# Moving small transfers of the projection to GpSimd's queue and queueing two jobs later in a hybrid attention / gMLP layer

## The chip, the core and the metric

The kernel runs on one core of a Trainium2 chip. The core has a matrix engine (TensorE, PE in the profile; its weight loads are PEld), a vector engine (VectorE, DVE), an activation engine (ScalarE, ACT), a general engine (GpSimd, POOL) and SyncE (SP), which here only issues transfers. Each engine takes its instructions in order, and engines wait for one another by semaphores. A transfer (DMA) is issued by an engine, stands in that engine's queue until its own conditions hold, and is then carried by 16 transfer engines that all queues share. The metric is the device time of one execution in microseconds (us).

## The reference

One layer for 2048 latent tokens and 256 context tokens, width 1024, all in float32. The part that matters here is the input projection and what is made of it:

```python
h_x = modulate(x, norm1_g[l], sh1, sc1)
p_x = h_x @ w_in[l]
k_x = apply_rope(rmsnorm(kv_heads(p_x[..., :K_W]), k_norm_g[l]), cos, sin)
v_x = kv_heads(p_x[..., K_W:KV_COLS])
q_x, u_x, vg_x, ga_x, gb_x = jnp.split(p_x[..., KV_COLS:], REST_SPLITS, axis=-1)
q_x = apply_rope(rmsnorm(q_heads(q_x), q_norm_g[l]), cos, sin) * q_scale
...
attn_x = merge_heads(attend_blocked(q_x, k_all, v_all))
gm_x = gmlp_spatial(jax.nn.gelu(u_x), jax.nn.gelu(vg_x), gm_norm_g[l], gm_ws[l], gm_bs[l])
x = x + g1 * branch_merge(attn_x, gm_x, ga_x, gb_x, w_br_attn[l], w_br_gm[l], w_out[l])
h2 = modulate(x, norm2_g[l], sh2, sc2)
x = x + g2 * sq_relu_mlp(h2, w_ff1[l], w_ff2[l])
```

The gMLP mixes 128-token chunks: `gmlp_spatial` normalizes v, multiplies each chunk by a 128 x 128 matrix per head group, adds a bias and multiplies by u.

## The kernel before

**Products.** Every float32 operand is split into a high part and a remainder (`split`, `operand`, `pair_chunk`): ScalarE casts the high part, VectorE subtracts. A product is three matmuls, high x high, high x low, low x high (lines L1742 to L1744). The large products are done with seven block products instead of eight, numbered p and taken in the order `SUMS = (0, 1, 5, 6, 4, 2, 3)`. Each output block is complete after one of the passes 1, 4, 2 or 3.

**Stages.** Projection (`project`, roughly the first 740 us), attention, merging of the branches, and the feed-forward layer. Only the projection is touched. There, the 2048 tokens are worked in two blocks (`blk` 0 and 1) of two 512-token quarters each (`b` = 2 blk and 2 blk + 1). Within a block come two column groups called pairs, pair 0 (keys, values, queries; 2 x 384 columns) and pair 1 (the gMLP's u and v; 2 x 512 columns), and eight gate groups. In block 0 the order is pair 0, gate groups 0 and 1, pair 1, gate groups 2 to 7; in block 1 both pairs and then all gates. `pairs_run` works a pair in 14 steps: seven passes p with two chunks of weights each, and in each step four tiles of 128 tokens. Weights of a step are loaded, cast and subtracted up to three steps ahead (L694 from the weights, L710 and L712, L713 from the stored differences `t_d`).

**What a pair leaves.** `Pair.leave` (L2115) writes each 128-token tile of an output block to HBM (`p_d`). If the block is a plain copy, ScalarE copies and issues the store (L2119, L2123). If an earlier part has to be added, VectorE makes the sum (L2121) into a buffer tagged `t2`, of which there are six, and SyncE issues the store (L2123). That is so for the passes 4 and 2.

**Small jobs.** What becomes of `p_d` is done by generators in a list, `self.work`; each turn (`tick`) advances the first job of the list to its next `yield`, so that the instructions of a job are strewn between those of the products. A job waits in the list until those before it are done. The jobs are: `keys_work` (load from `p_d`, norm L779, L780, L810, table L465 to L480, rotation L491 to L498, split L820, L821, transposes L192, store to `k_d` L834), `queries_work` (the same for queries, loads L842 to L844, L851), `mixing` (the gMLP; loads L871 and L896, split L157, load of the transposed mixing matrices `ws_d` L919, products L186, result to `gm_d`), `gm_consts` (L954 to L960, which makes `ws_d`), `terms` (weight differences of pair 1) and `h_ahead` (operands of block 1). `mixing` takes buffers tagged `m`, of which there are four, so the buffer for `ws_d` is one that the split L157 has just read. In block 0, a steered generator (`opening`) also runs `context_keys` from step 10 of pair 0 on: load of the context (L505), sums of squares (L515), reciprocal root on VectorE (`rsqrt`, L163 to L179), scaling (L528), transposes (L999), modulation (L1003), and its own small product.

**Which job comes when.** `Pair.begin` has a table `ends`: after which pass which jobs are appended. For pair 0 these are the first keys after pass 1, the first queries after pass 2, and the second keys and queries after pass 3. In block 0 no job gets a turn before step 9 of pair 0, which is part of pass 4, since the operand sums go first (`hold`). `terms` is inserted behind the job that is first in the list when the first pair ends, and must be done early in the second.

**Order on the engines.** The framework's planner orders the instructions of each engine in the projection by its own estimates of durations and by what each depends on; some stretches are pinned to the written order (`order`). All the loads of weights, the stores named above except ScalarE's, and the loads of the jobs are on SyncE's queue.

Of the kernel before, what the change touches and what calls it, by code (L numbers as in the profile page):

```python
# [72 lines left out]
class Kern:  # L73
# [387 lines left out]
    def rope_tables(self, w, b):  # L461
        nc = self.nc
        H = HD // 2
        cs = self.t1([TT, HD])
        nc.sync.dma_start(  # L465
            cs, self.I["rope"].rearrange("(t p) d -> p t d", p=P)[:, b * TT : (b + 1) * TT]
        )
        gb = self.rg[w].unsqueeze(1).broadcast_to([P, TT, HD])
        tab = self.t2([2, TT, HD])
        t1, t2 = tab[:, 0], tab[:, 1]  # L470
        cos, sin = cs[:, :, :H], cs[:, :, H:]
        for o in (0, H):
            nc.vector.tensor_tensor(
                out=t1[:, :, o : o + H], in0=cos, in1=gb[:, :, o : o + H], op=ALU.mult
            )
        nc.vector.scalar_tensor_tensor(
            out=t2[:, :, :H], in0=sin, scalar=-1.0, in1=gb[:, :, H:],
            op0=ALU.mult, op1=ALU.mult,
        )
        nc.vector.tensor_tensor(out=t2[:, :, H:], in0=sin, in1=gb[:, :, :H], op=ALU.mult)  # L480
        return t1, t2
# [317 lines left out]
    def keys_work(self, nt, b, kraw=None):  # L799
        nc = self.nc  # L800
        c = 0 if b is None else b + 1
        if b is not None:
            kraw = self.t2([TT, NKV, HD])
            nc.sync.dma_start(
                kraw.rearrange("p t h d -> p t (h d)"), self.rows(self.pr_d[0][b][0], slice(0, P))
            )
            yield
            yield
# [18 lines left out]
        for kv in range(NKV):  # L827
            ps = self.bank([TB])
            self.transposes(
                ps, [f32(kk[:, t, kv]).rearrange("p a d -> p (a d)") for t in range(nt)]  # L830
            )
            ka = self.t2([TB])
            nc.scalar.copy(ka[:, :n], ps[:, :n])
            nc.sync.dma_start(self.k_d[c][kv][:, :n], ka[:, :n])  # L834
        yield

    def queries_work(self, b):
# [3 lines left out]
        src = self.pr_d[0][b]  # L841
        nc.sync.dma_start(flat[0][:, :, :P], self.rows(src[0], slice(2 * P, 3 * P)))  # L842
        nc.sync.dma_start(flat[0][:, :, P:], self.rows(src[1], slice(0, P)))
        nc.sync.dma_start(flat[1], self.rows(src[1], slice(P, 3 * P)))  # L844
        yield
# [23 lines left out]
    def raw_values(self, b, j, c):  # L869
        x = self.m4([TT, 4, HD])  # L870
        self.nc.sync.dma_start(  # L871
            x.rearrange("p t g d -> p t (g d)"),
# [19 lines left out]
    def mixing(self, b, c):  # L892
        nc = self.nc
        v, u = (self.raw_values(b, j, c) for j in range(2))
        gn = self.t2([256])
        nc.sync.dma_start(  # L896
            gn,
# [20 lines left out]
        ws = self.m4([2, 4, P], F32R)  # L918
        nc.sync.dma_start(f32(ws).rearrange("p n g q -> p n (g q)"), self.ws_d[c])  # L919
        yield  # L920
# [29 lines left out]
    def gm_consts(self):  # L950
        nc = self.nc
        for c in range(2):
            w = self.t2([4, P])
            nc.sync.dma_start(w, self.I["gm_ws"][0, c * 4 : (c + 1) * 4].rearrange("g p q -> p g q"))  # L954
            ps = self.bank([TB])
# [3 lines left out]
            nc.vector.tensor_tensor(out=t[:, 1], in0=ps, in1=f32(t[:, 0]), op=ALU.subtract)  # L959
            nc.sync.dma_start(self.ws_d[c], f32(t))  # L960
            yield
# [1131 lines left out]
class Pair:  # L2093
# [6 lines left out]
    def begin(self, blk):  # L2100
        self.blk = blk
        k, b = self.k, 2 * blk
        if self.index == 0:
            self.ends = {
                1: lambda: [k.keys_work(TT, b)],
                2: lambda: [k.queries_work(b)],
                3: lambda: [k.keys_work(TT, b + 1), k.queries_work(b + 1)],
            }
# [6 lines left out]
    def leave(self, i, j, t, ps, u=None):  # L2115
# [6 lines left out]
        dst = k.pr_d[self.index][2 * self.blk + i][j]  # L2122
        (nc.scalar if u is None else nc.sync).dma_start(dst[t * P : (t + 1) * P, :], x)  # L2123

# [304 lines left out]
```

## Time and profile before

| what | us |
|---|---|
| median of 3 runs | 3018.83 (3016.13 to 3022.55) |
| the profiled execution | 3009.05 |
| its span, first to last instruction | 3007.2 |
| TensorE's idle time in the span | 75.6 |

How to read the profile: the page gives the busy time of each engine and its share of the span. A stretch row gives the same in a window of time, with the share of full speed that TensorE's clock was granted and the busy share of the transfer engines. A wait row reads "engine, tile, line <- the engine, tile and line that released it: total us, times, longest us". In a timeline row stand the start, the duration, the engine, the line, the operation and its tiles, and in brackets the idle time before it and what ended it. "SPq" is SyncE issuing a transfer; such rows merge neighbours of one line (x2), and a merged row's duration runs from the first to the last. Tile names have their buffer numbers left out; `t` stands for `t1`, `t2` and `t4`, and `p_d<-t` is a store of a sum. Landing times of transfers are not in this trace.

### The profile page before, as it was taken

The numbers are of one execution on the slowest core, as the hardware profiler recorded it, in microseconds if no ns is written. First come the engines' busy times: TensorE is split into PE (matmuls) and PEld (weight loads), VectorE is DVE, ScalarE is ACT, GpSimd is POOL, SyncE is SP. The second block draws the span as 40 slices with busy tenths as digits, with TensorE's granted clock in tenths as the row PEclk, the third lists the DMA queues.
The fourth block names the chain that finished last, engine by engine and source line by source line (L and its number), as shares of the span: only waits on it lengthen the run. The fifth ranks groups of instructions, "written<-read, shape, count | busy, mean of one in ns | idle before, by whom it ended". The sixth has DMA issues, their size and how long they took to land. (4 is left out here: it accounts for less than half of the span.)

```text
span 3007.2 us, 37935 instructions
## 1 busy us (share of the span) xinstructions
PE 2931.6 (97%) x13325; PEld 2206.7 (73%) x13325; DVE 2062.5 (69%) x2983; ACT 1417.9 (47%) x2318; POOL 652.8 (22%) x470
## 2 busy tenths in 40 slices
PE   7899999989999999999999989999999999999999
PEld 5778788876555555556888878888887888888887
DVE  5866487765788888867555587776676766654555
ACT  5554865553544545444222354444454344444432
POOL 0000000001999899894211200000000000000000
PEclk9999999999999999999999999999999999999999
DMA  7587866774010010016776658888766544447564
GB/s 276 184 295 272 307 215 217 256 247 140 24 36 26 25 37 22 22 36 191 238 215 194 183 198 308 307 305 303 261 219 224 186 154 154 154 154 277 210 209 155
DMA packets 386175, 559.04 MB, mean 186 GB/s; under 512 B 38640, under 2 KB 192416, under 8 KB 385984
## 3 DMA queue, kind: packets, MB, share of 16 engines
q1 hardware_dynamic: 373616, 535.89, 53.7%
q10 hardware_dynamic: 12368, 20.73, 1.8%
q8 instruction: 105, 1.72, 0.2%
q14 instruction: 86, 0.70, 0.1%
HBM read 379.75 MB, written 176.69 MB: 185 GB/s over the span
## 5 line engine op out<-in xcount | busy, mean ns | idle before, releaser
L2251 DVE TENSOR_REDUCE ts<-b 128x1 f32<-128x512 f32 x512 | 313.0, 681 | 75.3 <-PE b L2240 75.2
L2336 POOL TENSOR_TENSOR ac<-ac,p 128x512 f32<-128x512 f32 x214 | 306.3, 1463 | 50.5 <-ACT p L2308 50.5
L1858 DVE TENSOR_TENSOR b<-b,b 128x1024 fp32r<-128x1024 f32 x170 | 200.7, 1220 | 135.7 <-ACT b L1857 135.4
L1857 ACT CAST b<-b 128x1024 fp32r<-128x1024 f32 x170 | 170.6, 1050 | 222.2 <-PE b L1744 100.1
L2308 ACT ACTIVATE p<-b 128x512 f32<-128x512 f32 x384 | 194.1, 627 | 168.6 <-PE b L2304 168.1
L1743 PE MATMUL b<-b,b 128*128 128x512 f32 x680 | 265.2, 390 | 2.8 <-DVE b L1858 2.7
L1742 PE MATMUL b<-b,b 128*128 128x512 f32 x680 | 266.0, 391 | 1.6 <-DVE f L1879 1.4
L1744 PE MATMUL b<-b,b 128*128 128x512 f32 x680 | 264.7, 389 | 0.0
L2336 POOL TENSOR_TENSOR ac<-p,p 128x512 f32<-128x512 f32 x32 | 52.4, 1656 | 746.0 <-DMA raw<-in_w_mod 741.3
L2336 POOL TENSOR_TENSOR ac<-ac,t 128x512 f32<-128x512 f32 x152 | 205.0, 1378 | 0.0
L2285 PE MATMUL b<-h,h 128*128 128x512 f32 x576 | 188.0, 406 | 3.9 <-ACT p L2308 2.2
L2316 PE MATMUL b<-p,h 128*64 128x512 f32 x768 | 186.5, 609 | 0.0
L2304 PE MATMUL b<-h,h 128*128 128x512 f32 x576 | 179.1, 392 | 0.0
L1743 PE MATMUL b<-hb,b 128*128 128x512 f32 x446 | 173.8, 390 | 0.0
L1752 DVE TENSOR_TENSOR f<-f,b 128x512 f32<-128x512 f32 x160 | 109.0, 682 | 78.6 <-issue 45.8
L1742 PE MATMUL b<-hb,b 128*128 128x512 f32 x415 | 162.0, 390 | 0.3 <-DVE f L1752 0.3
L1744 PE MATMUL b<-hb,b 128*128 128x512 f32 x415 | 161.3, 389 | 0.0
L2285 PEld LDWEIGHTS b<-h,h 128*128 128x128 f32 x576 | 104.1, 189 | 65.1 <-DVE ts L2251 26.0
L1743 PEld LDWEIGHTS b<-b,b 128*128 128x128 f32 x680 | 127.6, 188 | 31.4 <-DVE b L1858 4.7
L1742 PEld LDWEIGHTS b<-b,b 128*128 128x128 f32 x680 | 127.6, 188 | 29.5 <-ACT b L1857 2.3
L1744 PEld LDWEIGHTS b<-b,b 128*128 128x128 f32 x680 | 127.7, 188 | 26.4
L157 POOL TENSOR_TENSOR bw<-bw,bw 128x512 fp32r<-128x512 f32 x58 | 75.8, 1328 | 235.7 <-ACT bw L153 235.7
(436 smaller groups left out, 7207.0 us busy)
## 6 DMA issues: line engine op xcount, KB each, us to landing
ao_d<-f SPq DMA_DIRECT2D x224, 256.0 KB
f<-in_w_ff SPq DMA_DIRECT2D x48, 1024.0 KB
b<-ao_d SPq DMA_DIRECT2D x85, 512.0 KB
b<-w2o_d SPq DMA_DIRECT2D x85, 512.0 KB
w2o_d<-f SPq DMA_DIRECT2D x112, 256.0 KB
f<-in_w_in SPq DMA_DIRECT2D x38, 512.0 KB
f<-x_d SPq DMA_DIRECT2D x64, 256.0 KB
hb<-ao_d SPq DMA_DIRECT2D x54, 256.0 KB
```

Of the source, the lines that this page charges most:

```text
L1742: mm(ps, wh, hh, start=start and k == 0, stop=False, skip_group_check=True)
L1743: mm(ps, wh, hl, start=False, stop=False, skip_group_check=True)
L1744: mm(ps, wl, hh, start=False, stop=k == len(w) - 1, skip_group_check=True)
L1752: nc.vector.tensor_tensor(out=out, in0=in0, in1=in1, op=op)
L1857: nc.scalar.copy(h, f32(l))
L1858: nc.vector.tensor_tensor(out=l, in0=f32(l), in1=f32(h), op=ALU.subtract)
L2251: nc.vector.tensor_reduce(out=self.mx[:, t, h, c : c + 1], in_=ps[h], axis=AX.X, op=ALU.max)
L2285: self.nc.tensor.matmul(self.pts[j][h], k.KA[c][self.kv][:, ks], self.qa[h], start=True, stop=False, skip_group_check=True,)
L2304: self.nc.tensor.matmul(s, k.KB[c][self.kv][:, ks], self.qb[h], start=False, stop=True, skip_group_check=True,)
L2308: self.nc.scalar.activation(pt[h], s, AF.Exp)
L2316: nc.tensor.matmul(self.o[h * HD : (h + 1) * HD, :], k.V[c][:, i, self.kv * HD : (self.kv + 1) * HD], pt[h], start=j == 0, stop=j == NKT - 1,)
L2336: nc.gpsimd.tensor_tensor(out=self.acc[e][:, h], in0=old[:, h], in1=pt[h], op=ALU.add)
```

## The change

Twelve places that issued on SyncE's queue now issue on GpSimd's: the rotation table, the loads for keys, for queries, for u and v and for the gMLP's norm, the load of the mixing matrices, the stores of keys, the two transfers of `gm_consts`, and the stores of VectorE's sums. That is 102 transfers in an execution: 32 stores of sums, 10 of keys and 2 of mixing matrices, and 58 loads. No transfer was issued by GpSimd before.

The table `ends` of pair 0 is written from a list of four jobs and the passes after which they are appended. In block 1 these are the passes of before (1, 2, 3, 3); in block 0 they are (2, 3, 3, 3): the first keys are appended after pass 2 in place of pass 1 and the first queries after pass 3 in place of pass 2, which are steps 11 and 13 of the 14 (numbered from 0) in place of 3 and 11.

```diff
     def rope_tables(self, w, b):
...
-        nc.sync.dma_start(
+        nc.gpsimd.dma_start(
             cs, self.I["rope"].rearrange("(t p) d -> p t d", p=P)[:, b * TT : (b + 1) * TT]
         )
...
     def keys_work(self, nt, b, kraw=None):
...
-            nc.sync.dma_start(
+            nc.gpsimd.dma_start(
                 kraw.rearrange("p t h d -> p t (h d)"), self.rows(self.pr_d[0][b][0], slice(0, P))
             )
...
-            nc.sync.dma_start(self.k_d[c][kv][:, :n], ka[:, :n])
+            nc.gpsimd.dma_start(self.k_d[c][kv][:, :n], ka[:, :n])
...
     def queries_work(self, b):
...
-        nc.sync.dma_start(flat[0][:, :, :P], self.rows(src[0], slice(2 * P, 3 * P)))
-        nc.sync.dma_start(flat[0][:, :, P:], self.rows(src[1], slice(0, P)))
-        nc.sync.dma_start(flat[1], self.rows(src[1], slice(P, 3 * P)))
+        nc.gpsimd.dma_start(flat[0][:, :, :P], self.rows(src[0], slice(2 * P, 3 * P)))
+        nc.gpsimd.dma_start(flat[0][:, :, P:], self.rows(src[1], slice(0, P)))
+        nc.gpsimd.dma_start(flat[1], self.rows(src[1], slice(P, 3 * P)))
...
     def raw_values(self, b, j, c):
...
-        self.nc.sync.dma_start(
+        self.nc.gpsimd.dma_start(
             x.rearrange("p t g d -> p t (g d)"),
...
     def mixing(self, b, c):
...
-        nc.sync.dma_start(
+        nc.gpsimd.dma_start(
             gn,
...
-        nc.sync.dma_start(f32(ws).rearrange("p n g q -> p n (g q)"), self.ws_d[c])
+        nc.gpsimd.dma_start(f32(ws).rearrange("p n g q -> p n (g q)"), self.ws_d[c])
...
     def gm_consts(self):
...
-            nc.sync.dma_start(w, self.I["gm_ws"][0, c * 4 : (c + 1) * 4].rearrange("g p q -> p g q"))
+            nc.gpsimd.dma_start(w, self.I["gm_ws"][0, c * 4 : (c + 1) * 4].rearrange("g p q -> p g q"))
...
-            nc.sync.dma_start(self.ws_d[c], f32(t))
+            nc.gpsimd.dma_start(self.ws_d[c], f32(t))
...
         if self.index == 0:
+            at = (1, 2, 3, 3) if blk else (2, 3, 3, 3)
+            jobs = [w for c in (b, b + 1) for w in (k.keys_work(TT, c), k.queries_work(c))]
             self.ends = {
-                1: lambda: [k.keys_work(TT, b)],
-                2: lambda: [k.queries_work(b)],
-                3: lambda: [k.keys_work(TT, b + 1), k.queries_work(b + 1)],
+                p: lambda p=p: [w for q, w in zip(at, jobs) if q == p] for p in set(at)
             }
...
     def leave(self, i, j, t, ps, u=None):
...
-        (nc.scalar if u is None else nc.sync).dma_start(dst[t * P : (t + 1) * P, :], x)
+        (nc.scalar if u is None else nc.gpsimd).dma_start(dst[t * P : (t + 1) * P, :], x)
```

## The prediction

> **What bounds the kernel now.** I read the page first, then the busy time by stretches of 30 us in the stage that the change touches (the projection, the first 740 us), then TensorE's waits there, and last the timeline of the one long wait.
>
> ```profile
> span 3007.2 us, 37935 instructions
> PE 2931.6 (97%) x13325; PEld 2206.7 (73%) x13325; DVE 2062.5 (69%) x2983; ACT 1417.9 (47%) x2318; POOL 652.8 (22%) x470
> ```
>
> TensorE is busy 97% of the span, so the whole idle time is 3007.2 - 2931.6 = 75.6 us, and no change of queues can win more than its part of that. The stretches (columns: length, then busy us and instructions of PE, weight loads, DVE, ACT, POOL; then granted clock, DMA share, GB/s):
>
> ```profile
> 90.00:120.00 30.00, 19.71 (x102) 18.09 (x103) 23.97 (x61) 14.93 (x25) 0.00 (x0) 0.83 0.63 196
> 120.00:150.00 30.00, 30.00 (x163) 25.61 (x162) 26.27 (x46) 18.29 (x30) 0.00 (x0) 1.00 0.60 183
> 150.00:180.00 30.00, 28.65 (x133) 23.00 (x132) 18.36 (x25) 11.72 (x19) 0.00 (x0) 1.00 0.89 319
> 180.00:210.00 30.00, 28.46 (x132) 23.32 (x132) 15.77 (x45) 15.05 (x27) 0.00 (x0) 1.00 0.94 311
> ```
>
> The reader is to see three things: TensorE loses 30 - 19.71 = 10.3 us in one stretch and 0 to 1.5 us in those behind it; the granted clock is 0.83 in that stretch alone; and VectorE has 26.27 of 30 us of work right behind it, but 18.36 and 15.77 later. TensorE's waits (who, for whom: total us, times, longest), the first from the view of 75 to 150 us, the others from that of 117 to 740 us:
>
> ```profile
> PE b L999 <- ACT m L528: 6.9, 2, 6.4
> ...
> PE b L186 <- DMA m<-ws_d: 5.2, 6, 1.5
> PE a L1742 <- ACT a L2176: 4.5, 4, 1.9
> PE b L192 <- DVE m L821: 1.9, 2, 1.5
> PE a L1742 <- ACT t L2178: 1.6, 1, 1.6
> ```
>
> One wait of 6.4 us stands out, and the only transfer that TensorE itself waits for is the load of the mixing weights (ws_d). The timeline around the long wait:
>
> ```profile
> 99.88 0.19 ACT L515 ACTIVATION_READ_ACCUMULATOR t<-m 128x1 f32 x1
> 103.08 0.16 DVE L163 TENSOR_SCALAR ts<-ts 128x2 f32<-128x2 f32 x1
> 104.94 0.69 DVE L498 TENSOR_TENSOR t<-t,t 128x512 f32<-128x512 f32 x1
> 105.93 0.83 ACT L712 CAST f<-f 128x768 fp32r<-128x768 f32 x1 [5.86 <-DMA f<-t_d]
> 106.79 0.96 DVE L713 TENSOR_TENSOR f<-f,f 128x768 fp32r<-128x768 f32 x1 [1.16 <-ACT f L712]
> 108.84 0.16 DVE L179 SCALAR_TENSOR_TENSOR ts<-ts,ts 128x2 f32<-128x2 f32 x1
> 109.09 2.19 ACT L528 ACTIVATE m<-m,ts 128x1024 f32<-128x1024 f32 x2 [0.76 <-DVE ts L179]
> 110.30 0.48 PE L999 MATMUL b<-ident,m 128*128 128x128 f32 x1 [6.37 <-ACT m L528]
> 111.33 0.48 PE L999 MATMUL b<-ident,m 128*128 128x128 f32 x1 [0.56 <-ACT m L528]
> 112.52 0.69 PE L999 MATMUL b<-ident,m 128*128 128x128 f32 x2 [0.71 <-ACT t L1003]
> 114.29 0.69 PE L1742 MATMUL a<-f,hx 128*128 128x384 f32 x1 [1.09 <-ACT a L734]
> ```
>
> Read backwards: TensorE's transposes of the context (L999) wait for the scaling (L528), that for the last step of a reciprocal root on VectorE (L179). The sums of squares were ready at 99.88 + 0.19 = 100.07, but the root's first step (L163) came at 103.08 and its last at 108.84. Two things lie between. One is the first keys' job, whose rotation (L498) runs until 105.6. The other is VectorE's in-order wait at L713 for ScalarE's L712, which waits 5.86 us for a weight load (f<-t_d). That load is late because SyncE issues it late:
>
> ```profile
> 93.86 0.33 SPq L2123 DMA_DIRECT2D p_d<-t  x1
> ...
> 95.99 3.07 SPq L2123 DMA_DIRECT2D p_d<-t  x2
> 99.15 0.39 SPq L1047 DMA_DIRECT2D f<-in_w_in  x1
> 99.59 0.72 SPq L710 DMA_DIRECT2D f<-t_d  x1
> ```
>
> Between 95.99 and 99.06 its queue holds two stores of VectorE's sums (L2123), the second issued only when its sum is made; the loads behind it go out at once afterwards, so they were ready earlier. Both causes are just what the diff moves.
>
> **The change part by part.**
>
> *A, the long wait.* The keys' job of block 0 leaves this place: it is now queued after the pass p = 2 rather than p = 1. Counted by the loops, its first step moves from step 9 to step 11 of the first pair. Some of what VectorE sheds ahead of the root:
>
> ```profile
> L498 DVE TENSOR_TENSOR t<-t,t 128x512 f32<-128x512 f32 x1 | 0.7, 692 | 0.0
> L810 DVE TENSOR_TENSOR t<-t,ts 128x512 f32<-128x512 f32 x1 | 0.7, 683 | 0.0
> ...
> L780 DVE TENSOR_REDUCE ts<-m 128x8 f32<-128x512 f32 x1 | 0.7, 679 | 0.0
> ```
>
> That is 692 + 683 + 679 ns = 2.05 us, and the job's table, the rest of its rotation and its own root come on top. The root could then start near 100.1 rather than 103.1. The load f<-t_d goes out up to 99.06 - 95.99 = 3.1 us earlier, so L712 ends near 103.7 rather than 106.8 and L528 can follow at once. TensorE reaches L999 at 110.30 - 6.37 = 103.93, so most of the 6.37 us is gone: I keep 1.0 of it. Of the three small waits behind it (0.56 + 0.71 + 1.09 = 2.36 us) I keep half, since they come from ScalarE's and VectorE's alternation, which stays. The clock comes on top:
>
> ```profile
> 107.20:117.40 10.20, 4.75 (x15) 3.76 (x16) 8.03 (x19) 6.17 (x9) 0.00 (x0) 0.50 0.25 80
> ```
>
> It is at half speed for 10.2 us, beginning 3.3 us after the idle time began; 4.75 us of matmuls in it would take half as long at full speed, so 2.4 us. Sum of A: 5.4 + 1.2 + 2.4 = -9.0 us; bounds 0 (the load lands no earlier and takes the whole chain with it) to -(6.37 + 2.36 + 2.4) = -11.1.
>
> The Trainium skill's page "TensorE: Matmul & The Clock Gate" (Part 1) says that the gate knows half and full speed only and needs some 3.4 us of busy time to open again. The trace agrees on the two values; by that figure alone the clock would be worth about 1.7 us in place of 2.4, an estimate.
>
> *B, SyncE's queue.* 102 transfers leave it: 32 stores of sums, 12 of keys and mixing weights, and 58 loads for the small jobs. Its waits in the projection for two of them alone:
>
> ```profile
> SPq L2123 <- DVE t L2121: 41.4, 22, 6.4
> ...
> SPq L919 <- DVE m L157: 21.0, 8, 7.8
> ```
>
> Weight loads queued behind these go out earlier. But no wait of TensorE's beyond ws_d is for a transfer: weights are first cast by ScalarE, and what TensorE can feel of a late one is a wait for a ScalarE copy that stands behind the cast, L2176 and L2178 (4.5 + 1.6 = 6.1 us). I take half, -3.0; bounds 0 and -6.1.
>
> *C, the load of the mixing weights.* It cannot start before VectorE's L157 has freed a buffer, and TensorE waits for it:
>
> ```profile
> 444.43 1.22 DVE L157 TENSOR_TENSOR m<-m,m 128x1024 fp32r<-128x1024 f32 x1
> ...
> 445.68 0.32 SPq L919 DMA_DIRECT2D m<-ws_d  x1
> ...
> 449.66 0.38 PE L186 MATMUL b<-m,m 128*128 128x256 f32 x1 [0.90 <-DMA m<-ws_d]
> ```
>
> L157 ends at 445.65 and the issue follows in 0.03 us: SyncE's queue costs this load nothing, so GpSimd's can only be slower. From issue to use are 3.98 us. No transfer in this trace is issued by GpSimd, so its extra time is bounded by 0 and by half of those 3.98 us; I take 0.5, near the low end because the issue row itself is 0.32 us. With the 6 waits that are already exposed: +3.0 us, bounds 0 and +12.
>
> The Trainium skill's page "DMA: Bandwidth & Descriptors" (Specifications) gives about 1 us to the first byte from GpSimd's queue and 0.6 from SyncE's or ScalarE's. By it C would be 6 x 0.4 = 2.4 us, an estimate; no run here shows it yet.
>
> *D, the jobs in their new place.* The keys' job runs beside the last three steps of the first pair, and the queries' job of block 0 leaves the stretch 120:150 and comes behind the context's keys and the mixing constants, by the count of steps in 150:180 and 180:210. There VectorE has 11.6 and 14.2 idle us. From the pass p = 2 of the second pair on, nothing is late: in the kernel before, the loops' turns for jobs ran empty ahead of that point, and these turns take up the delay. I take one more wait of the kind L192 <- L821: +1.0, bounds 0 and +4. If VectorE were not idle there, the queries' full-width work would stand in line with the sums, and the upper bound would hold.
>
> *E, buffers.* Sums, keys and tables share six t2 buffers, which a store holds until it has landed. A slower store gives them back later: +1.0, with the upper end in the first rival.
>
> Sum: -9.0 - 3.0 + 3.0 + 1.0 + 1.0 = -7.0 us. The profiled execution took 3009.05 us (span 3007.2 and 1.85 around it), so 3002.0; the median of the runs shown is 9.8 us above it, and against that median the forecast is 3018.8 - 7.0 = **3011.8 us**.
>
> **The rivals.**
>
> *First, GpSimd's queue cannot keep up (slower).* The stores come in bursts:
>
> ```profile
> 435.06 0.89 SPq L2123 DMA_DIRECT2D p_d<-t  x2
> ...
> 446.14 0.81 SPq L2123 DMA_DIRECT2D p_d<-t  x2
> ```
>
> Eight of them lie between 435.06 and 446.95, 1.5 us apart. Six buffers cover some 6 x 1.5 = 9 us more. If one transfer occupies GpSimd's queue for over (11.9 + 9) / 8 = 2.6 us, VectorE waits for a buffer, TensorE's bank is not emptied, and TensorE waits. At 3.2 us, 8 x 3.2 - 20.9 = 4.7 us in each of four bursts: +19, so 3031. Against it: GpSimd has 0.00 us of other work in every stretch shown. For it: the loads for keys and queries are cut into 512 rows each, the stores into 128.
>
> The Trainium skill's "SBUF — State Buffer" (the "DVE blocks DMA" trap) supplies a mechanism: GpSimd's descriptors cannot be written while VectorE runs in a two-port mode. Rows that bear on it:
>
> ```profile
> 114.58 0.42 DVE L155 CAST m<-t 128x512 fp32r<-128x512 f32 x1
> ...
> 115.52 0.68 DVE L157 TENSOR_TENSOR m<-t,m 128x512 fp32r<-128x512 f32 x1
> ```
>
> Only the cast runs at a higher rate than the subtractions of the same size, and the moved jobs are mostly of the second kind, so I give this little weight.
>
> *Second, A does not come.* The transfer engines were nearly full while the late load was under way:
>
> ```profile
> 98.00:104.00 6.00, 5.71 (x32) 5.07 (x30) 5.69 (x26) 2.07 (x4) 0.00 (x0) 1.00 0.95 287
> ```
>
> With a share of 0.95 an earlier issue may only wait elsewhere: f<-t_d lands at 105.9 as before, and L528 still stands behind L712 on ScalarE. Then A shrinks to the 2.3 us between 106.8 and 109.1, with 1 us of the clock and of the small waits -3.3, and the sum to -1.3: 3017.5.
>
> *Third, B is larger.* All 6.1 us of B go, C costs nothing, and some of the many waits under 1 us with it: 3011.8 - 3.1 - 3.0 = 3005.7, and some 3003 with them. For it: the 41.4 us above. Against it: TensorE's waits are already short.
>
> **How the numbers follow.** Chances: forecast 0.45 (3005 to 3018 by itself), first rival 0.20, second 0.20, third 0.15. Faster by over 0.2% means under 3012.8, slower over 3024.9; 0.2% is about what a measurement of this kernel tells from no change. Faster: the third rival and about 0.33 of the forecast, 0.48. Slower: the first rival, 0.20. The rest, 0.32. The range runs from 2999 (third rival with A at its bound, D and E at nothing: 3003 - 2.1 - 1.0 - 1.0) to 3031.
>
> **What would show it.** Right: the clock stays at 1.00 between 100 and 120 us, L999 waits under 2 us, no L2123 of VectorE's sums on SyncE's queue, and the wait for ws_d grows by 2 to 4 us in total. Wrong: L712 still ends near 106.8 (second rival); VectorE's L2121 waits for transfers (first rival); new TensorE waits for queries' or keys' transposes near 180 us (D). The planner may also order instructions anew in the whole projection; waits that appear there in other lines would be that, and I have no row to price it.

## The result and the profile after

The changed kernel takes 3067.09 us (median of 5 runs, 3063.50 to 3068.69) and the kernel before, in the same comparison, 3020.50 us (5 runs, 3016.13 to 3022.55). The ratio is 1.0156, with a 95% interval of 1.0145 to 1.0167: 46.6 us slower, where 7.0 us faster was forecast. The time lies 36 us above the upper end of the range.

The page of the changed kernel:

```profile
span 3066.9 us, 37997 instructions
PE 2957.8 (96%) x13325; PEld 2227.7 (73%) x13325; DVE 2065.2 (67%) x2983; ACT 1419.6 (46%) x2318; POOL 717.5 (23%) x572
...
q0 software_dynamic: 9248, 31.20, 3.2%
```

TensorE's busy time rose by 26.2 us though it runs the same 13325 matmuls, and a queue of another kind (`software_dynamic`, GpSimd's: packets, MB, share) now carries 31.20 MB. To see where the time went, the span is cut at the same place of both programs, where the first matmul of line L2304 starts, early in the attention: at 739.5 us before and at 798.0 us after. Stretches of the kernel before, then of the changed one (columns as in the prediction's stretches):

```profile
0.00:739.50 739.50, 685.00 (x3280) 555.55 (x3281) 496.41 (x938) 414.54 (x685) 0.70 (x6) 0.99 0.73 243
739.50:3007.20 2267.70, 2246.57 (x10046) 1651.14 (x10044) 1566.08 (x2045) 1003.34 (x1633) 652.12 (x464) 1.00 0.50 167
```

```profile
0.00:798.00 798.00, 709.96 (x3280) 575.51 (x3281) 497.63 (x938) 416.28 (x685) 65.52 (x108) 0.96 0.68 225
798.00:3066.90 2268.90, 2247.84 (x10046) 1652.16 (x10044) 1567.61 (x2045) 1003.36 (x1633) 651.95 (x464) 0.99 0.50 167
```

The second parts differ by 1.2 us, so the loss is all in the projection: 58.5 us. Of these 58.5 us, 33.5 us are idle time of TensorE (798.00 - 709.96 = 88.0 against 739.50 - 685.00 = 54.5) and 25.0 us are the same 3280 matmuls taking longer (709.96 - 685.00), with the granted clock at 0.96 in place of 0.99. The traces differ by more than the medians because the profiled execution of before was 11.5 us under its median and that of after 1.6 us above its own.

TensorE's waits in the changed kernel, from 75 to 790 us (who, for whom: total us, times, longest):

```profile
PE b L186 <- DMA m<-ws_d: 16.3, 7, 3.2
PE a L1742 <- ACT t L2178: 10.1, 3, 5.9
PE a L1742 <- ACT a L2176: 7.0, 2, 6.3
```

The three lines that the prediction used for its parts B and C stand at the top, and they grew: ws_d from 5.2 to 16.3 us, the copies L2176 and L2178 from 6.1 to 17.1 us. The long wait at L999, in turn, is gone. Its timeline:

```profile
99.80 0.19 ACT L515 ACTIVATION_READ_ACCUMULATOR t<-m 128x1 f32 x1
100.02 0.17 DVE L163 TENSOR_SCALAR ts<-ts 128x2 f32<-128x2 f32 x1
...
102.20 0.16 DVE L179 SCALAR_TENSOR_TENSOR ts<-ts,ts 128x2 f32<-128x2 f32 x1
102.46 1.16 ACT L528 ACTIVATE m<-m,ts 128x1024 f32<-128x1024 f32 x1 [2.47 <-DVE ts L179]
...
105.02 0.27 PE L999 MATMUL b<-ident,m 128*128 128x128 f32 x1
```

The root starts 0.03 us after the sums of squares are ready (99.99) and the transposes start without a wait. So the change did what it says at 104 us, and lost far more elsewhere.

What the copies L2176 and L2178 wait for begins in GpSimd's own timeline. In its rows stand the start, the time that issuing takes, and in brackets the idle time before it. The loads for queries, and those of u and v:

```profile
188.17 0.77 POOL L842 DMA_DIRECT2D m<-p_d  x1 [0.37 <-PE b L192]
192.16 0.77 POOL L843 DMA_DIRECT2D m<-p_d  x1 [3.23 <-issue]
192.92 0.56 POOL L960 DMA_DIRECT2D ws_d<-m  x1
196.61 0.76 POOL L844 DMA_DIRECT2D m<-p_d  x1 [3.13 <-issue]
203.24 0.75 POOL L465 DMA_DIRECT2D t<-in_rope  x1 [5.87 <-issue]
...
367.30 0.76 POOL L871 DMA_DIRECT2D m<-p_d  x1 [78.51 <-PE b L192]
373.96 0.77 POOL L871 DMA_DIRECT2D m<-p_d  x1 [5.90 <-DMA tb_d<-t]
```

"issue" means that nothing in the trace holds the instruction back. For transfers of this queue the view of the transfers gives the us from issue to landing (last column); for L842 and L844, each alone in its window:

```profile
m<-p_d POOLq DMA_DIRECT2D x1, 256.0 KB, 3.7
...
m<-p_d POOLq DMA_DIRECT2D x1, 512.0 KB, 6.3
```

L842 landed at 188.17 + 3.7 = 191.9, and L843 was issued at 192.16. L844 landed at 196.61 + 6.3 = 202.9, and L465 was issued at 203.24. A load cut into 512 rows goes out some 0.3 us after the 512-row load before it has landed, while the store of 128 rows at L960 follows L843 at once. The second L871 goes out 0.34 us after the first has landed, at 373.62; its row names a store, tb_d<-t, that ended within 0.01 us of that landing. What follows from that at 374 us, on ScalarE and TensorE:

```profile
381.92 1.15 ACT L882 ACTIVATE t<-m 128x512 f32<-128x512 f32 x2 [5.54 <-DMA m<-p_d]
...
383.49 0.56 ACT L2178 COPY t<-a 128x512 f32<-128x512 f32 x1
...
384.11 0.79 PE L1742 MATMUL a<-h,f 128*128 128x512 f32 x1 [5.91 <-ACT t L2178]
```

ScalarE stands 5.54 us at L882 for the load issued at 373.96. The copy L2178, queued behind it, empties TensorE's bank late, and TensorE stands for 5.91 us.

This is not the only place. In the changed kernel eight of TensorE's waits for ScalarE, 27.2 us together, end within 5.5 us after ScalarE has stood over 0.8 us for a load from `p_d` at L779 or L882; the kernel before has none. All of TensorE's waits behind 75 us in the projection grew from 35.0 to 68.7 us. These eight, the 11.1 us more for ws_d and the 6.9 us that are gone at L999 make 31.4 of the 33.7 us.

### The profile page after: what moved, and what is told of

Its sections match the earlier page's. It is cut to its first block, busy times and chain, and to the rows that moved or that the text cites. A ratio compares the mean times of both kernels' runs of the same rounds, so it can differ in the third digit from the quotient of the medians.

```text
span 3066.9 us, 37997 instructions
## 1 busy us (share of the span) xinstructions
PE 2957.8 (96%) x13325; PEld 2227.7 (73%) x13325; DVE 2065.2 (67%) x2983; ACT 1419.6 (46%) x2318; POOL 717.5 (23%) x572
## 3 DMA queue, kind: packets, MB, share of 16 engines
q0 software_dynamic: 9248, 31.20, 3.2%
## 4 chain that ended last, share of the span: by engine, by line
PE 77%; issue 9%; DMA 4%; DVE 3%; ACT 1%; POOL 1%; SPq 0%; ACTq 0%; POOLq 0%; DVEq 0%
PE b L1742 13%; PE b L1743 13%; PE b L1744 13%; PE b L2316 9%; PE b L2285 5%; PE b L2304 4%; PE b L186 4%; PE b L187 4%; PE b L188 4%; PE b L2240 3%; PE a L1742 1%; PE a L1743 1%; PE a L1744 1%; DMA m<-ws_d 1%; DMA m<-p_d 1%
## 5 line engine op out<-in xcount | busy, mean ns | idle before, releaser
L2304 PE MATMUL b<-h,h 128*128 128x512 f32 x576 | 179.9, 394 | 0.0
L1743 PEld LDWEIGHTS b<-b,b 128*128 128x128 f32 x680 | 127.7, 188 | 31.4 <-DVE b L1858 4.7
L157 POOL TENSOR_TENSOR bw<-bw,bw 128x512 fp32r<-128x512 f32 x58 | 75.3, 1321 | 236.2 <-ACT bw L153 236.2
L1742 PE MATMUL a<-f,h 128*128 128x384 f32 (+1 forms) x320 | 118.5, 376 | 11.1 <-ACT a L727 5.4
```

The lines of the kernel that those rows point to most:

```text
L1742: mm(ps, wh, hh, start=start and k == 0, stop=False, skip_group_check=True)
L1743: mm(ps, wh, hl, start=False, stop=False, skip_group_check=True)
L2304: self.nc.tensor.matmul(s, k.KB[c][self.kv][:, ks], self.qb[h], start=False, stop=True, skip_group_check=True,)
```

## The experiments

Four theories were put against each other. The **ring** theory (R): the kernel reserves 1024 bytes for the descriptors of GpSimd's transfers (an argument at L2415), a 512-row load leaves no room for another, and the next one must wait. The **latency** theory (L): each transfer from GpSimd's queue is slower, and TensorE feels it at ws_d. The theory of the **stores held up** (H): the sums' stores wait in GpSimd's queue and VectorE's buffers run out (the prediction's first rival). The theory of the planner's **order** (P): what costs is not the queue but the new order of the instructions, because of the later jobs or because GpSimd's queue is in use. All ratios are to the kernel before timed beside the run, with 95% intervals; its median lay between 3012.91 and 3020.50 us, so ratios are compared and not times.

### The change taken in two

`order_only`: only the later jobs, all transfers on SyncE's queue.

```diff
+            at = (1, 2, 3, 3) if blk else (2, 3, 3, 3)
+            jobs = [w for c in (b, b + 1) for w in (k.keys_work(TT, c), k.queries_work(c))]
             self.ends = {
-                1: lambda: [k.keys_work(TT, b)],
...
+                p: lambda p=p: [w for q, w in zip(at, jobs) if q == p] for p in set(at)
             }
```

> The later jobs of block 0 alone, every transfer on SyncE's queue as before. Theories of the loss of 47 us: R, a transfer of 512 rows does not fit beside another one in GpSimd's descriptor ring and waits until that one has landed; H, GpSimd's one in-order queue holds the stores of sums behind loads that wait for buffers; L, every transfer from GpSimd takes longer from issue to landing, and TensorE waits for it at ws_d and ScalarE at u and v; P, the planner's new order of the engines, not the queue itself. R, H and L: this run has none of the loss and keeps the gain of the long wait at 104 us, 3008 to 3016, the wait for L999 under 1.5 us. P, if the later jobs are its cause: 3040 or more.

`queue_only`: only the queue, with the jobs of before in both blocks.

```diff
-            at = (1, 2, 3, 3) if blk else (2, 3, 3, 3)
+            at = (1, 2, 3, 3)
```

> The queue alone, the jobs of block 0 as before. R, H and L: 3060 to 3085, since the loss is the queue's, with ws_d waits of 12 us or more in total. P, with the later jobs as its cause: 3015 to 3030. If the long wait at 104 us goes here too, the freed queue of SyncE was its cause and not the keys' job; I expect it to shrink to 3 us but not to go.

Measured: `order_only` 3017.33 us, 1.0005 (0.9995 to 1.0016), and `queue_only` 3075.84 us, 1.0192 (1.0173 to 1.0210). The queue carries the whole loss, and the later jobs alone give no gain that can be measured, where 3008 to 3016 us were expected. With the transfers on GpSimd's queue they do gain: the change stands at 1.0156, `queue_only` at 1.0192, and the intervals do not meet. So the two parts do not simply add up, and the prices below hold with the later jobs in place. `queue_only` also tells which half of the prediction's part A was right. TensorE's waits from 75 to 130 us there, and then ScalarE's timeline:

```profile
PE b L999 <- ACT m L528: 10.4, 2, 9.9
```

```profile
101.12 0.63 ACT L779 ACTIVATE m<-t 128x512 f32<-128x512 f32 x1 [3.23 <-DMA t<-p_d]
...
103.65 0.19 ACT L515 ACTIVATION_READ_ACCUMULATOR t<-m 128x1 f32 x1
...
107.30 0.83 ACT L712 CAST f<-f 128x768 fp32r<-128x768 f32 x1 [2.74 <-DMA f<-t_d]
...
113.27 2.19 ACT L528 ACTIVATE m<-m,ts 128x1024 f32<-128x1024 f32 x2 [3.67 <-DVE ts L179]
```

The stores have left SyncE's queue, and ScalarE's wait for f<-t_d falls from 5.86 to 2.74 us, yet TensorE waits 9.9 us, longer than before. Part of that is the new queue: ScalarE stands 3.23 us for the keys' load, and the sums of squares are ready at 103.84 us, 3.8 us later than before. But from there to L528 are 9.4 us, against 9.0 before, so with the keys' job in its old place the earlier f<-t_d shortened nothing. `order_only` is the other half, by its waits of TensorE and its timeline of ScalarE:

```profile
PE b L999 <- ACT t L1003: 2.5, 1, 2.5
```

```profile
106.46 0.83 ACT L712 CAST f<-f 128x768 fp32r<-128x768 f32 x1 [2.28 <-DMA f<-t_d]
```

The load f<-t_d is as late there as before (L712 at 106.46 us against 105.93), and the wait for L528 is gone all the same. What stays are 2.5 us for L1003, which stands behind that L712 on ScalarE.

### Which transfers

`stores_only`: later jobs, and only the 32 stores of sums on GpSimd's queue; `loads_only`: the change, with these 32 back on SyncE's.

```diff
 # stores_only: every transfer of the change but this one on nc.sync
-        (nc.scalar if u is None else nc.sync).dma_start(dst[t * P : (t + 1) * P, :], x)
+        (nc.scalar if u is None else nc.gpsimd).dma_start(dst[t * P : (t + 1) * P, :], x)
```

> The later jobs, and of the 102 transfers only the 32 stores of sums on GpSimd's queue (128 rows each, six or seven fit the ring). R, H and L: nothing waits for a ring, no store stands behind a load, and no load lands later: 3010 to 3022, equal to the later jobs alone within 6 us. P, now as: the planner orders worse as soon as GpSimd's queue is in use: 3035 or more.

```diff
 # loads_only: against the changed kernel
-        (nc.scalar if u is None else nc.gpsimd).dma_start(dst[t * P : (t + 1) * P, :], x)
+        (nc.scalar if u is None else nc.sync).dma_start(dst[t * P : (t + 1) * P, :], x)
```

> The opposite: all loads for the jobs and the stores of keys on GpSimd's queue, the stores of sums on SyncE's. H (the stores of sums are held up and with them the t2 buffers) says that most of the loss goes: 3020 to 3040. R and L say that it stays: 3055 to 3080, with ws_d waits of 12 us or more and waits of L882 for u and v of 20 us or more.

Measured: `stores_only` 3020.28 us, 1.0022 (1.0012 to 1.0033), and `loads_only` 3063.84 us, 1.0163 (1.0147 to 1.0179), the same as the change. The stores are nearly free, and held-up stores fall as a cause. P falls as far as the later jobs alone and the stores alone can show it.

`small_loads_sp`: the change, with every transfer of 512 rows back on SyncE's queue. `ws_small_sp`: the load of ws_d back as well. `mix_sp`: the change, with the gMLP's three loads back.

```diff
 # small_loads_sp: L465, L804, L842 to L844, L871, L954, each like this
-        self.nc.gpsimd.dma_start(
+        self.nc.sync.dma_start(
             x.rearrange("p t g d -> p t (g d)"),
```

> The changed kernel with the seven kinds of transfers of 512 rows back on SyncE's queue (table, keys, queries, u and v, and the mixing matrices' first load); stores, the ws_d loads, the norm's rows and the keys' stores stay on GpSimd's. R: no issue follows 0.3 us behind a landing, and at least the 20 us that the larger ring gave come back; with the faster landing of u, v, keys and queries 3025 to 3045. L for ws_d alone: its waits stay at 12 to 16 us against 5 to 7. If it stays over 3055, R and L together are wrong.

```diff
 # ws_small_sp: against small_loads_sp
-        nc.gpsimd.dma_start(f32(ws).rearrange("p n g q -> p n (g q)"), self.ws_d[c])
+        nc.sync.dma_start(f32(ws).rearrange("p n g q -> p n (g q)"), self.ws_d[c])
```

> The run with the 512-row transfers back on SyncE's queue, with the eight ws_d loads back there too; left on GpSimd's queue are the stores of sums and of keys, the store of ws_d and the norm's rows. L at ws_d: the waits for ws_d fall from 15.9 to 5 to 7.5 us and the time by 8 to 13 us, to about the run with the stores alone, ratio 1.001 to 1.004. If the remaining loss lies in sharing one queue and not in the landing of ws_d, the ratio stays at 1.005 or more.

```diff
 # mix_sp: against the changed kernel, L871, L896 and L919, each like this
-        nc.gpsimd.dma_start(
+        nc.sync.dma_start(
             gn,
```

> The changed kernel with only the gMLP's transfers (u, v, norm, ws_d) back on SyncE's queue. If the loss lies in the mixing jobs, by L at ws_d (16.3 us of waits against 5.2) and by R and L at u and v (29.5 us of waits on ScalarE against 4.8): 3025 to 3042. If it lies with keys and queries: over 3050.

Measured:

| kernel | of the small transfers on GpSimd's queue | us | ratio |
|---|---|---|---|
| `order_only` | none | 3017.33 | 1.0005 (0.9995 to 1.0016) |
| `ws_small_sp` | all stores, loads of the norm | 3017.97 | 1.0009 (1.0000 to 1.0018) |
| `small_loads_sp` | those and the loads of ws_d | 3030.72 | 1.0054 (1.0039 to 1.0068) |
| `mix_sp` | all but the loads of u, v, norm, ws_d | 3030.85 | 1.0058 (1.0045 to 1.0072) |
| the change | those and the 512-row transfers | 3067.09 | 1.0156 (1.0145 to 1.0167) |

Read down without `mix_sp`, each row adds one group, and its price is the difference of the ratios times 3018 us: the stores and other small ones 1 us (5 us by `stores_only`, whose interval overlaps), the loads of ws_d 14 us, the 512-row transfers 31 us. The planner's order moves along with each row: at least 227, 285 and 423 of the 13325 places in TensorE's order hold another instruction than in the row above, so a price is that of the transfers with the order that came of moving them. In `small_loads_sp` none of TensorE's waits stands behind a late load from `p_d` as the eight of the changed kernel do. `mix_sp` agrees from the other side: without the gMLP's loads 30 us of the loss are gone.

For ws_d, TensorE's waits in `small_loads_sp` and then in `ws_small_sp`:

```profile
PE b L186 <- DMA m<-ws_d: 15.9, 6, 4.8
```

```profile
PE b L186 <- DMA m<-ws_d: 4.2, 6, 1.2
```

The wait follows the queue of that one load alone: 11.7 us of waits and 13.6 us of time for 8 loads. One of them in the changed kernel, by its timelines of VectorE, GpSimd and TensorE:

```profile
396.15 1.23 DVE L157 TENSOR_TENSOR m<-m,m 128x1024 fp32r<-128x1024 f32 x1
...
397.67 0.55 POOL L919 DMA_DIRECT2D m<-ws_d  x1 [22.40 <-DMA t<-h_d]
...
404.21 0.36 PE L186 MATMUL b<-m,m 128*128 128x256 f32 x1 [3.13 <-DMA m<-ws_d]
```

From the end of L157 (397.38) to the use are 6.8 us, where the prediction's example of the kernel before took 4.01 us (445.65 to 449.66). Over the seven loads behind the first, which nobody waits for, the mean from issue to use is 5.55 us against 4.76, and the issue follows L157 after 0.30 us in place of 0.03.

### The ring

Two kernels were made to differ in the reserved bytes alone. The memory for more bytes had to come from somewhere, so both give up one buffer of two pools.

```diff
 # both, against the changed kernel
-    "front": {"hx": 16, "f4": 10, "m": 4, "e2": 3},
-    "mid": {"p2": 8, "ac": 4},
+    "front": {"hx": 16, "f4": 9, "m": 4, "e2": 3},
+    "mid": {"p2": 7, "ac": 4},
 # pools_ring1792 alone
-    nc = bacc.Bacc("TRN2", target_bir_lowering=False, num_devices=1, dynamic_dma_scratch_size=1024)
+    nc = bacc.Bacc("TRN2", target_bir_lowering=False, num_devices=1, dynamic_dma_scratch_size=1792)
```

> Control for the next run: the changed kernel with one buffer less of f4 and of p2, which makes room for a larger ring but leaves the ring at 1024 bytes. All theories: near the changed kernel, 3065 to 3085 (the two buffers cost 0 to 15 us).

> The same instructions in the same order on every engine as the control, ring of 1792 in place of 1024 bytes, room for three transfers of 512 rows. R: the issues that follow 0.3 us behind a landing become rare (14 in the changed kernel, 3 or fewer here), and the time falls by 15 to 40 us against the control. H and L: the issues move, but the time stays within 6 us of the control.

Measured: 3081.75 us with 1024 bytes, 1.0219 (1.0201 to 1.0238), and 3062.29 us with 1792, 1.0151 (1.0133 to 1.0170). The instructions stand in the same order on every engine in both, so the 19.5 us are the reserved bytes alone. (The lost buffers, with the order that came of them, have a price of their own: 1.0219 against 1.0156 for the change. The larger reserve with fewer buffers, at 1.0151, is no cure.) GpSimd's timeline with 1792 bytes, at the two places shown above:

```profile
182.75 0.77 POOL L842 DMA_DIRECT2D m<-p_d  x1 [0.34 <-issue]
183.51 0.77 POOL L843 DMA_DIRECT2D m<-p_d  x1
...
187.72 0.75 POOL L844 DMA_DIRECT2D m<-p_d  x1 [2.89 <-PE a L1744]
...
360.88 0.76 POOL L871 DMA_DIRECT2D m<-p_d  x1 [78.19 <-DMA h_d<-t]
364.24 0.76 POOL L871 DMA_DIRECT2D m<-p_d  x1 [2.61 <-PE b L192]
```

L843 now follows L842 in 0.76 us, with no idle time, in place of 3.99 us in the changed kernel, and the second L871 follows the first in 3.36 us in place of 6.66. Counted over the projection, 17 of the 512-row transfers went out 0.30 to 0.37 us after the landing of the 512-row transfer issued just before them, in the changed kernel as with 1024 bytes, and none with 1792; there three followed so on one issued three transfers earlier. ScalarE's waits for these loads from 120 to 790 us, first in the kernel before, then with 1024 bytes, then with 1792:

```profile
ACT t L882 <- DMA m<-p_d: 4.8, 6, 2.2
```

```profile
ACT t L882 <- DMA m<-p_d: 28.7, 11, 5.8
```

```profile
ACT t L882 <- DMA m<-p_d: 15.0, 11, 2.8
```

The longest falls from 5.8 to 2.8 us, and TensorE's waits behind such loads fall from 24.4 to 12.0 us. If the pair's 19.5 us carry over to the change, the ring theory stands for some 20 of the 31 us. What the 512-row loads cost beyond it (1792 bytes still held three issues back, and ScalarE still waits 15.0 us against 4.8) wasn't separated further.

The Trainium skill's page "DMA: Bandwidth & Descriptors" (SWDGE vs HWDGE vs iDMA) says that GpSimd writes the descriptors of its transfers to rings in a part of SBUF set aside for them, and that transfers issued by SyncE or ScalarE never use these. That agrees with the pair of runs, where the size of that part alone made 19.5 us. The same page of the Trainium skill (Issuing engines are not separate DMA queues) says that issuing from several engines only saves issue time; here the change of the engine alone, `queue_only`, stands at 1.0192, and the measurement decides.

### Where the gain of the later jobs went

`order_only` lost the wait at L999 and won nothing. A second trace of the kernel before and one of `order_only` were taken, unchanged, because the profiled execution of before lies 11.5 us under its median.

> The kernel before, unchanged, for a second trace: its first profiled execution took 3009.05 us, 11 us under the median of its runs, so all comparisons of traces with it carry that difference. If an execution near the median loses those 11 us in the projection (a varying landing of transfers, waits at other places, then the clock at half speed), its first attention product starts near 748 to 751 us in place of 739.5, and the loss of the later jobs in the stretch of 200 to 260 us is partly chance. If the projection ends near 739.5 again and the 11 us lie behind it, the stretch 200 to 260 us keeps about 59 us of TensorE's work, and the 4.4 us wait for the second queries' rotation is the order's own.

> The later jobs with all transfers on SyncE's queue, unchanged, for a second trace. If the wait for the second queries' rotation (L192 for L498) belongs to the order, it is there again with over 3 us near 249 us, and TensorE is busy about 52 of the 60 us from 200 to 260. If it was chance, it is under 1.5 us and the stretch has 57 us or more. The wait at L999 stays under 3 us either way.

The first took 3015.78 us and the second 3016.30 us, one execution each. They reach the cut of above at 743.8 and 745.7 us. The first lies between its two expectations, and against it the projection of the changed kernel loses 54.2 us in place of 58.5. Stretches and waits of the kernel before, second trace:

```profile
90.00:120.00 30.00, 20.30 (x107) 18.96 (x107) 23.59 (x62) 14.77 (x26) 0.00 (x0) 0.83 0.60 190
200.00:260.00 60.00, 57.43 (x267) 46.70 (x266) 44.87 (x80) 30.44 (x46) 0.00 (x0) 1.00 0.71 235
```

```profile
PE b L999 <- ACT m L528: 7.6, 2, 7.0
```

The same of the later jobs, with one more stretch:

```profile
90.00:120.00 30.00, 24.59 (x133) 23.45 (x132) 23.08 (x47) 18.32 (x31) 0.00 (x0) 0.89 0.70 215
200.00:260.00 60.00, 52.53 (x240) 42.36 (x239) 50.52 (x93) 26.05 (x40) 0.00 (x0) 0.94 0.59 191
...
240.00:250.00 10.00, 3.11 (x16) 2.08 (x15) 10.00 (x13) 1.46 (x3) 0.00 (x0) 0.85 0.14 40
```

```profile
PE b L192 <- DVE m L498: 4.5, 1, 4.5
...
PE a L1742 <- ACT a L734: 2.7, 1, 2.7
```

Both waits are in both traces of their kernel (L999: 6.4 and 7.0 us; L192 for L498: 4.4 and 4.5 us, ending at 249 and 246 us), so they belong to the order. The later jobs win 4.3 us of TensorE's work in the first stretch and lose 4.9 us in the second, where VectorE is busy 10.00 of 10 us. There the rotation of the second queries (L498), put off, meets pair 1's sums and weights, and TensorE's transposes wait for it. The gain is given back 140 us later.

Five more kernels tried to put that work elsewhere. `late_q1` moves the second queries' job of block 0 between the two mixing jobs, `late_kq1` the second keys' with it, and `q1_only` leaves the other jobs as before.

```diff
 # late_q1: against order_only
-            at = (1, 2, 3, 3) if blk else (2, 3, 3, 3)
+            at = (1, 2, 3, 3) if blk else (2, 3, 3, 9)
...
+            late = [] if blk else [k.queries_work(b + 1)]
...
-                2: lambda: [k.mixing(b, c) for c in range(2)],
+                2: lambda: [k.mixing(b, 0)] + late + [k.mixing(b, 1)],
```

> All on SyncE's queue and the later jobs of block 0, but the second queries' job of block 0 moved on, behind the first mixing job. Theory of why the later jobs alone gained nothing: the 9 us won at 104 us are lost again at 245 to 256 us, where that job's rotations now meet pair 1's sums on VectorE. Then this run keeps the gain: ratio 0.9965 to 0.999, no wait of L192 for L498 over 1.5 us near 250 us. If the loss is in the planner's order as a whole, 1.000 to 1.003.

```diff
 # late_kq1: against late_q1
-            at = (1, 2, 3, 3) if blk else (2, 3, 3, 9)
+            at = (1, 2, 3, 3) if blk else (2, 3, 9, 9)
-            late = [] if blk else [k.queries_work(b + 1)]
+            late = [] if blk else [k.keys_work(TT, b + 1), k.queries_work(b + 1)]
```

> As the run before, with the second keys' job moved there as well. Same theory: ratio 0.996 to 0.999, VectorE with a little more room at 200 to 245 us. If moving work into the time of the mixing jobs costs there, 1.000 to 1.004 with new waits behind 400 us.

```diff
 # q1_only: against late_q1
-            at = (1, 2, 3, 3) if blk else (2, 3, 3, 9)
+            at = (1, 2, 3, 3) if blk else (1, 2, 3, 9)
```

> The jobs of before, all on SyncE's queue, with only the second queries' job moved behind the first mixing job. The long wait at 104 us must stay (6 us or more at L999), so the ratio is 0.999 to 1.002; if it falls below 0.998, the gain of the two runs before is not that of the keys' job.

`catch_gates` gives the list five extra turns in the gate groups 0 and 1 of block 0, and `catch_pair` five in the first steps of pair 1, so that the delay is made up before it meets pair 1's sums.

```diff
 # catch_gates: against order_only
-            self.tick(1 + (both and at > 4))
+            self.tick(1 + (both and at > 4) + (n == 2 and at > 2))
```

> All on SyncE's queue, the later jobs of block 0, and five extra turns for the list of jobs in the two first gate groups, so that the second queries' job starts in the same step of pair 1 as before the change. If the gain at 104 us is lost through that job's meeting with pair 1's sums at 245 us: ratio 0.996 to 0.999, no wait of L192 for L498 over 2 us and a first use of attention's values at 728 to 737 us. If the later jobs cost elsewhere too: 0.9995 to 1.003.

```diff
 # catch_pair: against order_only
-            self.tick()
+            self.tick(1 + (direct is None and len(pairs) == 1 and at < 5))
```

> The same with the five extra turns in the first five steps of pair 1 instead. Same theory: 0.996 to 0.999; as the turns fall where VectorE is busier than in the gates, up to 0.001 above the other run.

| kernel | us | ratio | TensorE's longest wait |
|---|---|---|---|
| `late_q1` | 3042.44 | 1.0097 (1.0084 to 1.0111) | 20.4 us for ws_d, at 707 us |
| `late_kq1` | 3059.23 | 1.0146 (1.0133 to 1.0160) | 19.9 us for ws_d, at 723 us |
| `q1_only` | 3050.76 | 1.0123 (1.0108 to 1.0139) | 19.3 us for ws_d, at 715 us; L999 5.9 us |
| `catch_gates` | 3030.94 | 1.0044 (1.0028 to 1.0059) | 17.2 us for L498, at 210 us |
| `catch_pair` | 3029.92 | 1.0038 (1.0023 to 1.0053) | 16.6 us for L498, at 208 us |

All five are slower. In the first three the wait for L498 is short, and a mixing job stands alone at the end of the projection. VectorE's and SyncE's timelines of `late_q1` there:

```profile
701.58 1.22 DVE L157 TENSOR_TENSOR m<-m,m 128x1024 fp32r<-128x1024 f32 x1 [1.11 <-ACT m L153]
```

```profile
702.84 0.32 SPq L919 DMA_DIRECT2D m<-ws_d  x1
```

TensorE waited from 687 to 707 us, but the load went out only at 702.84, 0.04 us after VectorE's split. So the wait that is put down to a transfer is mostly one for VectorE. In the last two, TensorE waits some four times longer for the rotation than in `order_only`. The planner's order changes in each of them: against `order_only`, at least 1700 to 2400 places of TensorE's order hold another instruction in the first three, and some 300 in the last two. Whether its order or the place of the job makes these waits stays open, and no version was found that beats the kernel before.

## Why the prediction was wrong

- **A, the long wait: right in its effect, half right in its cause.** The wait at L999 went from 6.37 us to under 1 us, and to 2.0 and 2.5 us for L1003 in the two traces of `order_only`. The keys' job was the cause of the long wait: in `order_only` it is gone with f<-t_d as late as before, and in `queue_only` it stays with f<-t_d earlier. SyncE's late issue stands for the 2.0 to 2.5 us at L1003, which are 0.7 us in the changed kernel. The clock did not stay at 1.00 between 100 and 120 us, as the sign asked: it was 0.74 before and 0.91 after. The second rival ("A does not come") is out.
- **B, SyncE's queue freed: no gain in time.** `ws_small_sp` takes 44 stores and 8 loads off SyncE and stands at 1.0009 against 1.0005 for `order_only`. TensorE's waits for the copies L2176 and L2178 do shorten, from 6.1 us before and 4.6 in `order_only` to 3.8 in `ws_small_sp` and 2.2 in `small_loads_sp`, but other waits took their place. The third rival is out with it.
- **C, the load of ws_d: right in its mechanism, mis-sized.** +3.0 us was taken, from 0.5 us each and 6 waits. Measured are 11.7 us of waits and some 14 us of time, at the upper bound of 12 and past it. The value near the low end was taken because the issue row is 0.32 us, but an issue row doesn't hold what the queue adds between issue and landing. The Trainium skill's figure in "DMA: Bandwidth & Descriptors" (Specifications) gave an estimate of 2.4 us, 0.4 us a load, and the traces don't agree with it as the price of a load: over the seven loads the mean is 0.27 us later to issue and 0.79 us longer to use, 1.06 us for each.
- **The step that failed: the loads of the jobs were priced at nothing.** Part B looked at ScalarE's place between a transfer and TensorE ("a wait for a ScalarE copy that stands behind the cast"), but only for what weights could gain. The same path was not walked for the 58 moved loads: u, v, keys and queries are read by ScalarE first (L882, L779), and TensorE's copies stand in line behind those. The 512-row transfers cost 31 us, and the eight waits behind ScalarE's late loads, 27.2 us, show the path. The first rival came near with its remark on the 512 rows, but put the price on the stores and on VectorE's buffers. `stores_only` at 1.0022 and `loads_only` at 1.0163 show the reverse. The lock between VectorE and GpSimd that the rival names was not tested by any run; GpSimd's issue rows, 0.54 to 0.56 us for each of the eight loads of ws_d, give no sign of it.
- **D, the jobs in their new place: mis-sized.** +1.0 us with an upper end of 4 was the term; in `order_only` it took all that A gave, some 9 us by the forecast and 4.3 us of TensorE's work in the traces. The stretch around 240 us, where VectorE was nearly full already in the kernel before (9.93 of 10 us from 230 to 240), was not priced: the sentence on empty turns let the delay end in the second pair, and the waits ahead of that point were taken as one short one.
- **E, buffers: nothing measurable.** VectorE's L2121 waits for no transfer in the changed kernel, and the stores cost about nothing.
- **The clock.** Only A was given a price for it. The 33.5 us of new gaps cost 58.5 us with the half clock behind them (granted clock 0.96 in place of 0.99), 1.7 times their length.

By the ratios, and with the later jobs in place, the change is made of +1.5 us for the order, +1 for the stores, +14 for ws_d and +31 for the 512-row transfers.

## What to carry to other kernels

Before a load is moved to another engine's queue, follow it to its first reader and to whatever stands in line behind that reader on the same engine, for losses as much as for gains. A queue with a small reserve for descriptors, like GpSimd's here with 1024 bytes, can take one many-row load at a time, so loads on whose landing an engine waits stay where they are issued side by side. Stores of few rows cost little on such a queue, but moving them gained nothing here either. Work put off to clear one wait needs a stretch where its engine is free all the way to the place where its result is used; look at the last such place, not only at the new first one.

## What was not expected of the hardware

- A transfer of 512 rows on GpSimd's queue holds the next one of 512 rows back until it has landed (0.3 us after), when 1024 bytes are reserved; one of 128 rows follows at once (L960 at 192.92 us). With 1792 bytes the first two of 512 rows go out 0.76 us apart. The 768 bytes are worth 19.5 us.
- Issuing takes GpSimd 0.77 us for 512 rows and 0.54 us for 128, while SyncE's rows in the kernel before have medians of 0.37 to 0.58 us for the same 512-row transfers and 0.32 us for ws_d.
- The 20 loads of 512 KB for u, v and queries took 6.1 us from issue to landing (median), up to 7.9 us in the example at 374 us.
